# Moving the two-input elementwise operations of a decoder layer's two mixers and of its rotary rotation from GpSimd to VectorE

## The chip, the core and the metric

The kernel runs on one core of one Trainium2 chip. The metric is device time in microseconds (us) of one execution, smaller is better; the time of a kernel is the median of its runs. A core has TensorE (PE: matmuls; PEld is its weight load), VectorE (DVE), ScalarE (ACT), GpSimd (POOL) and SyncE (SP, which issues the DMAs here). Each engine works through its own queue of instructions in order and waits on semaphores where an instruction needs another engine's result.

## The reference

One layer of a hybrid decoder over 2048 tokens of width 1024, with 16 meta tokens ahead of them, batch 1, all float32. Cut to what matters:

```python
u = rmsnorm(h, norm_mix_w); proj = u @ w_in
gq, gk, gv, gr, glr, sq, sk, sv = split(proj)
o_gla = gla_mixer(gq, gk, gv, gr, glr, ...)     # 4 heads, dk 64, dv 128
o_swa = swa_mixer(sq, sk, sv, sinks, pos)       # 8 heads of 64, 2 kv heads, window 128
h = h + concat([o_gla, o_swa]) @ w_out
h = h + square(relu(rmsnorm(h, norm_ff_w) @ w_ff1)) @ w_ff2
out = rmsnorm(h, final_norm_w)[:, 16:]
# gla_mixer, per chunk, with b = cumsum(log_sigmoid(gate)) / 16:
A[i, j] = sum_d q[i, d] * k[j, d] * exp(b[i, d] - b[j, d])   for j <= i
o = A @ v + (q * exp(b)) @ S;   S = exp(b_last) * S + (k * exp(b_last - b)).T @ v
o = rmsnorm(o) * silu(r)
# swa_mixer: rotary on the first 16 of 64 dims of q and k, then
# softmax over meta tokens + window + a sink per head
xr = xr * cos + rot(xr) * sin
```

## The kernel before, in words

Everything large is a matmul in three passes: `mm3` (L158 to L162) multiplies high part by high part, low by high and high by low. Each weight tile is split by `split_w` (L119): a DMA into `raw`, the high part `wh` by ACT (L125), the low part `wl` by DVE (L126). The token axis is cut into four blocks of 512 columns.

The dense work is a Python generator: `in_proj` twice (projections of two blocks each, with the rotation in `rope`, L199), then `trunk` for blocks 0 and 1 (output projection and feed-forward), then `tail_pair`, a hand-ordered stage for blocks 2 and 3 that does not touch the mixers. `drive` (after each yield of the dense generator) takes one step of each of two further generators: `gla` (the gated linear attention, 16 chunks of 128 tokens) and `swa` (sliding-window attention, 16 blocks of 128 queries). The mixers thus run beside the matmuls of `in_proj` and `trunk`. Ahead of `tail_pair` the order in which instructions stand on each engine is set by a scheduler from these streams and the tile pools; it is not written out by hand.

A GLA chunk (`gla_chunk`) turns the gates into a running sum `B` (DVE scan, L580), makes `qkp = q*k` (L695) and from it the diagonal `dg`, spreads that into `AT` (four POOL instructions, L705), and then goes through seven levels of block sizes 64 to 1. A level (`gla_level`) makes `E = B - B[at the block's middle]` (L659), two exponentials of its halves on ACT (L660, L661), the scaled keys `kl` (L663) and the scaled queries `ql` (DVE, L667). `gla_level_mm` multiplies them into PSUM (`lv`, L677, four matmuls with the weight loads counted apart) and copies the wanted entries into `AT` (DVE, L682). There are two `E`, two `kl` and two `ql` buffers. After the levels come `qB = q*exp(B)` (L717), the decayed keys `kt` (L587 to L589, in the second `kl` buffer), the state update, and the gate `sg` of the output (L762).

The attention takes scores in PSUM tiles `sc` (two buffers, tag `sx`, shared with transposes and norms), DVE adds the mask and takes the maximum (L471, which also writes `sst`), ACT takes exponentials (L479), POOL divides by the sum (L494), PE transposes (L510), POOL masks two tiles (L523), PE multiplies by the values (L530, `pv`).

The rotation in `rope` swaps rows by a DVE shuffle into `sw` (L203), multiplies `sw` by the sine (L204), `raw` by the cosine (L205) and adds (L206); the feature is then stored by a DMA on the SP queue (L246).

The functions that the diff touches and what calls them:

Of the kernel before, what the change touches and what calls it, by code (L numbers as in the profile page):

```python
# [13 lines left out]
ALU = mybir.AluOpType  # L14
# [3 lines left out]
P = 128  # L18
# [17 lines left out]
class Layer:  # L36
# [162 lines left out]
    def rope(self, sp, raw, cs, n):  # L199

        nc = self.nc
        sw = sp.tile([P, NB], F32, name="sw", tag="sw", bufs=1)[:, :n]
        nc.vector.stream_shuffle(sw, raw, [(q + 8) % 16 if q < 16 else q for q in range(32)])  # L203
        nc.gpsimd.tensor_tensor(sw, sw, cs[:, 1, :], ALU.mult)  # L204
        nc.vector.tensor_tensor(raw, raw, cs[:, 0, :], ALU.mult)  # L205
        nc.vector.tensor_tensor(raw, raw, sw, ALU.add)  # L206
# [376 lines left out]
    def decayed_keys(self, gp, B, k, n):  # L583

        nc = self.nc
        kt = self.kl[1][:, :, :n]
        nc.gpsimd.tensor_tensor(kt, B[:, :, n - 1 : n].to_broadcast([P, 2, n]), B, ALU.subtract)  # L587
        nc.scalar.activation(kt, kt, AF.Exp, scale=1.0 / 16.0)
        nc.vector.tensor_tensor(kt, kt, k, ALU.mult)  # L589
        return kt  # L590
# [55 lines left out]
    def gla_level(self, li, gp, B, k):  # L646
        nc = self.nc
# [3 lines left out]
        def view(t):  # L651
            return t.rearrange("p a (n two s) -> p (a n) two s", two=2, s=s)


        flat = lambda t: t.rearrange("p a (n w) -> p (a n) w", w=2 * s)
        c = flat(B)[:, :, s - 1 : s].to_broadcast([P, 2 * nb, 2 * s])
        E = gp.tile([P, 2, P], F32, name="E", tag="E", bufs=2)
        Ev = view(E)
        nc.gpsimd.tensor_tensor(flat(E), flat(B), c, ALU.subtract)  # L659
        nc.scalar.activation(Ev[:, :, 0, :], Ev[:, :, 0, :], AF.Exp, scale=-1.0 / 16.0)  # L660
        nc.scalar.activation(Ev[:, :, 1, :], Ev[:, :, 1, :], AF.Exp, scale=1.0 / 16.0)  # L661
        kl = self.kl[li % 2]
        nc.gpsimd.tensor_tensor(view(kl)[:, :, 0, :], view(k)[:, :, 0, :], Ev[:, :, 0, :], ALU.mult)  # L663
        ql = gp.tile([P, 2, 2, 64], F32, name="ql", tag="ql", bufs=2)
# [22 lines left out]
    def gla_chunk(self, b, gp, qk, v):  # L687
        nc = self.nc
# [5 lines left out]
        qkp = gp.tile([P, 2, P], F32, name="qkp", tag="E", bufs=2)  # L694
        nc.gpsimd.tensor_tensor(qkp, q, k, ALU.mult)  # L695
        yield
# [19 lines left out]
        qB = gp.tile([P, 2, P], F32, name="qB", tag="qB", bufs=1)  # L716
        nc.gpsimd.tensor_tensor(qB, q, eB, ALU.mult)  # L717
        kt = self.decayed_keys(gp, B, k, P)
# [26 lines left out]
        for hp in range(2):  # L745
            for h in range(2):
                rr = slice(64 * h, 64 * h + 64)
                c = hp * 256 + h * P
# [12 lines left out]
        nc.scalar.activation(sg, sg, AF.Exp)  # L761
        nc.gpsimd.tensor_tensor(sg, sg, rf, ALU.mult)  # L762
        yield
# [916 lines left out]
```

## Time and profile before

| | |
|---|---|
| median of 3 runs | 2222.23 us (2220.12 to 2222.93) |
| profiled execution | 2224.15 us, of which the span from first to last instruction is 2222.1 us |
| granted TensorE clock, mean | 0.992 |
| ACT busy | 1049.8 us, 47% of the span, 2156 instructions |
| POOL busy in 40 slices of 55.6 us | 2042232644433344443310000000000000000001 |
| DMA | 291.47 MB, 131 GB/s mean |
| core's largest POOL group | L659, 112 instructions, 86.1 us |

How to read it: busy is the time in which an engine had an instruction running; the share of it in the span is an average over stages that differ. The slices show where in the span an engine works: POOL does nearly all of its work in the first 21 of 40 slices, which is where the two mixers run, that is up to about 1150 us. Only the last two normalisations use it after that.

In a group's row the numbers behind the bar are the busy time of the group, the mean duration of one instruction in ns, the idle time of the engine ahead of them, and what ended it. In a row of the timeline stand the start in us, the duration in us, engine, line, operation, output<-inputs, and, in brackets, how long the engine had been idle before and what released it. A row of a table of stages has the stretch, its length, and per engine the busy us with the count of instructions, then the granted clock (1.00 is full), the share of the DMA engines and GB/s.

### The profile page before, as it was taken

To read this page: it belongs to the slowest core of one execution; us is meant where nothing else is said; L and a number is where in the kernel's file an instruction comes from. 1 tells how busy PE (TensorE), PEld (TensorE's weight loads), DVE (VectorE), ACT (ScalarE), POOL (GpSimd) and SP (SyncE) were. 2 spreads that over 40 slices of the span, in tenths; PEclk is the share of its full clock that TensorE was granted. 3 is DMA by queue.
4 is the path that set the end of the run, shared out by engine and by line. 5 is a ranking of instruction groups with operands and counts; after the bars stand their busy time and mean duration, and the time that the engine had idled before them with its cause. 6 is when DMAs were issued, how large, how long until landed. Compare 5 with 4: busy or idle time off the path is not lost.

```text
span 2222.1 us, 29409 instructions
## 1 busy us (share of the span) xinstructions
PE 2160.2 (97%) x10423; PEld 1808.9 (81%) x10423; DVE 1530.8 (69%) x2617; ACT 1049.8 (47%) x2156; POOL 432.8 (19%) x621
## 2 busy tenths in 40 slices
PE   8999999989999999999999999999999999999997
PEld 6997789778788888887788888888788887888886
DVE  6166763878877777877975445556867776775866
ACT  5133754446665555656653233443455544333434
POOL 2042232644433344443310000000000000000001
PEclk9999999999999999999999999999999999999999
DMA  6333533325233333333533333563355456744412
GB/s 203 97 102 128 157 100 105 98 88 187 88 108 103 106 106 93 98 107 104 170 95 92 102 96 111 175 197 115 127 175 169 155 182 253 266 168 146 155 42 76
DMA packets 146802, 291.47 MB, mean 131 GB/s; under 512 B 12256, under 2 KB 63968, under 8 KB 146656
## 3 DMA queue, kind: packets, MB, share of 16 engines
q1 hardware_dynamic: 146656, 289.61, 40.7%
q8 instruction: 82, 1.34, 0.2%
q14 instruction: 64, 0.52, 0.1%
HBM read 219.63 MB, written 69.86 MB: 130 GB/s over the span
## 4 chain that ended last, share of the span: by engine, by line
PE 82%; DVE 9%; ACT 3%; POOL 3%; issue 2%; DMA 1%; DVEq 0%; SPq 0%; POOLq 0%; ACTq 0%
PE psd L162 15%; PE psd L160 15%; PE psd L161 15%; PE psq L160 4%; PE psq L162 4%; PE psq L161 4%; PE psw L160 4%; PE psw L162 4%; PE psw L161 4%; PE lv L677 2%; PE psd L295 2%; PE psd L296 1%; PE psd L297 1%; PE pv L530 1%; DVE wl L126 1%
## 5 line engine op out<-in xcount | busy, mean ns | idle before, releaser
L125 ACT ACTIVATE wh<-raw 128x1024 fp32r<-128x1024 f32 (+2 forms) x190 | 199.0, 1048 | 318.7 <-PE psd L162 275.9
L126 DVE TENSOR_TENSOR wl<-raw,wh 128x1024 fp32r<-128x1024 f32 (+2 forms) x190 | 239.7, 1262 | 99.5 <-ACT wh L125 98.5
L160 PE MATMUL psd<-hid,wh 128*128 128x512 f32 x512 | 205.0, 400 | 2.0 <-ACT hid L843 2.0
L1312 POOL TENSOR_TENSOR o<-acc,rb 128x256 f32<-128x256 f32 (+1 forms) x6 | 6.5, 1108 | 1019.1 <-DVE rb L85 1007.7
L160 PE MATMUL psd<-f,wh 128*128 128x512 f32 x512 | 202.7, 396 | 0.0
L162 PE MATMUL psd<-hid,wh 128*128 128x512 f32 x512 | 200.9, 392 | 0.0
L161 PE MATMUL psd<-hid,wl 128*128 128x512 f32 x512 | 200.7, 392 | 0.0
L162 PE MATMUL psd<-f,wh 128*128 128x512 f32 x512 | 199.9, 391 | 0.0
L161 PE MATMUL psd<-f,wl 128*128 128x512 f32 x512 | 199.7, 390 | 0.0
L160 PE MATMUL psd<-u,wh 128*128 128x512 f32 x416 | 170.0, 409 | 4.1 <-DVE st L241 2.4
L162 PE MATMUL psd<-u,wh 128*128 128x512 f32 x416 | 165.9, 399 | 0.6 <-DVE u L156 0.5
L161 PE MATMUL psd<-u,wl 128*128 128x512 f32 x416 | 165.1, 397 | 1.2 <-DVE wl L126 1.0
L160 PE MATMUL psw<-bh,wh 128*128 128x512 f32 x392 | 153.2, 391 | 2.2 <-DVE su L1195 2.2
L162 PE MATMUL psw<-bl,wh 128*128 128x512 f32 x392 | 153.2, 391 | 0.0
L161 PE MATMUL psw<-bh,wl 128*128 128x512 f32 x392 | 153.1, 391 | 0.0
L161 PE MATMUL psq<-oh,wl 128*128 128x512 f32 x384 | 149.5, 389 | 0.8 <-DVE wl L963 0.8
L162 PE MATMUL psq<-ol,wh 128*128 128x512 f32 x384 | 149.7, 390 | 0.6 <-DVE ol L913 0.6
L160 PE MATMUL psq<-oh,wh 128*128 128x512 f32 x384 | 149.8, 390 | 0.0
L962 ACT ACTIVATE wh<-rw 128x1024 fp32r<-128x1024 f32 x49 | 52.0, 1061 | 150.6 <-PE psw L162 134.3
L863 DVE TENSOR_TENSOR h<-h,psd 128x512 f32<-128x512 f32 x112 | 76.5, 683 | 61.2 <-PE psd L162 61.1
L160 PEld LDWEIGHTS psd<-hid,wh 128*128 128x128 f32 x512 | 97.1, 190 | 21.8 <-ACT hid L843 2.4
L162 PEld LDWEIGHTS psd<-hid,wh 128*128 128x128 f32 x512 | 96.7, 189 | 21.1 <-DVE hid L844 0.4
(315 smaller groups left out, 5494.4 us busy)
## 6 DMA issues: line engine op xcount, KB each, us to landing
raw<-w SPq DMA_DIRECT2D x132, 512.0 KB, 3.6
b<-hops SPq DMA_DIRECT2D x49, 512.0 KB, 3.6
raw<-wo SPq DMA_DIRECT2D x32, 512.0 KB, 4.0
r<-w SPq DMA_DIRECT2D x32, 512.0 KB, 4.1
rw<-w2q SPq DMA_DIRECT2D x28, 512.0 KB, 5.5
raw<-wf SPq DMA_DIRECT2D x26, 512.0 KB, 3.7
feat<-st SPq DMA_DIRECT2D x52, 256.0 KB, 2.0
hops<-t SPq DMA_DIRECT2D x42, 256.0 KB, 5.0
```

The source lines that it names most:

```text
L125: nc.scalar.activation(wh, raw, AF.Copy)
L126: nc.vector.tensor_tensor(wl, raw, wh.bitcast(F32), ALU.subtract)
L160: nc.tensor.matmul(ps, lhsT=wh, rhs=ah, start=first, stop=False, skip_group_check=skip)
L161: nc.tensor.matmul(ps, lhsT=wl, rhs=ah, start=False, stop=False, skip_group_check=skip)
L162: nc.tensor.matmul(ps, lhsT=wh, rhs=al, start=False, stop=last, skip_group_check=skip)
L295: nc.tensor.matmul(ps, lhsT=ah, rhs=wh, start=kt == 0, stop=False)
L296: nc.tensor.matmul(ps, lhsT=ah, rhs=wl, start=False, stop=False)
L297: nc.tensor.matmul(ps, lhsT=al, rhs=wh, start=False, stop=kt == KT - 1)
L530: nc.tensor.matmul(pv, lhsT=v[:, kv, :], rhs=t, start=i == 0 and t is ph, stop=False)
L677: nc.tensor.matmul(ps[:, hp * P : (hp + 1) * P], lhsT=kl[:, hp, :], rhs=ql[:, :, hp, :], start=True, stop=True)
L863: nc.vector.tensor_tensor(hs[m], hs[m], ps, ALU.add)
L962: nc.scalar.activation(wh, src, AF.Copy)
```

## The change

Seven places change their engine from `nc.gpsimd` to `nc.vector`; nothing else changes:

```diff
 rope:          (L204)
-        nc.gpsimd.tensor_tensor(sw, sw, cs[:, 1, :], ALU.mult)
+        nc.vector.tensor_tensor(sw, sw, cs[:, 1, :], ALU.mult)
 decayed_keys:  (L587)
-        nc.gpsimd.tensor_tensor(kt, B[:, :, n - 1 : n].to_broadcast([P, 2, n]), B, ALU.subtract)
+        nc.vector.tensor_tensor(kt, B[:, :, n - 1 : n].to_broadcast([P, 2, n]), B, ALU.subtract)
 gla_level:     (L659, L663)
-        nc.gpsimd.tensor_tensor(flat(E), flat(B), c, ALU.subtract)
+        nc.vector.tensor_tensor(flat(E), flat(B), c, ALU.subtract)
-        nc.gpsimd.tensor_tensor(view(kl)[:, :, 0, :], view(k)[:, :, 0, :], Ev[:, :, 0, :], ALU.mult)
+        nc.vector.tensor_tensor(view(kl)[:, :, 0, :], view(k)[:, :, 0, :], Ev[:, :, 0, :], ALU.mult)
 gla_chunk:     (L695, L717, L762)
-        nc.gpsimd.tensor_tensor(qkp, q, k, ALU.mult)
+        nc.vector.tensor_tensor(qkp, q, k, ALU.mult)
-        nc.gpsimd.tensor_tensor(qB, q, eB, ALU.mult)
+        nc.vector.tensor_tensor(qB, q, eB, ALU.mult)
-        nc.gpsimd.tensor_tensor(sg, sg, rf, ALU.mult)
+        nc.vector.tensor_tensor(sg, sg, rf, ALU.mult)
```

On POOL stay the copies into `qpad` (L692, L693), the diagonal `AT` (L705), the division `p` (L494), the masks `ph` and `pl` (L523), twelve adds of the first norms (L94) and a quarter of the last normalisation (L1312).

The scheduler lays the streams anew: POOL goes from 433 rows to 145 (a row can stand for several like instructions), DVE from 2420 to 2716, and the order on PE, ACT and SP changes in places up to the end of the mixers.

First place: the start of the levels of one chunk, in the second `in_proj` (275 us in the trace of before). On POOL before, two mask instructions, the diagonal, two `E`, the gate `sg`, and then the first `kl` of the chunk:

```order
L523 AFFINE_SELECT ph<-ph 128x512
L523 AFFINE_SELECT pl<-pl 128x512
L705 TENSOR_SCALAR AT<-tabs,dg 128x128 x4
L659 TENSOR_TENSOR E<-B 128x256 x2
L762 TENSOR_TENSOR sg<-sg,r 128x512
L663 TENSOR_TENSOR kl_122<-qk,E 128x2x64
L717 TENSOR_TENSOR qB<-qk,eB 128x256
L663 TENSOR_TENSOR kl_123<-qk,E 128x4x32
```

On POOL now the same stretch holds the masks and the diagonal alone, and the next masks follow at once. On DVE at that place (`st` is the evacuation of a projection, `acc` the sum of squares of the next block's norm), the difference is:

```order
 L241 SCALAR_TENSOR_TENSOR st<-psd,rb 128x512
-L243 TENSOR_TENSOR st<-psd,rb 128x512
-L94 TENSOR_TENSOR acc<-acc,sq 128x512
-L667 TENSOR_TENSOR ql<-qpad,E 128x256
-L94 TENSOR_TENSOR acc<-acc,sq 128x512
+L659 TENSOR_TENSOR E<-B 128x256
+L243 TENSOR_TENSOR st<-psd,rb 128x512
+L659 TENSOR_TENSOR E<-B 128x256
+L663 TENSOR_TENSOR kl_122<-qk,E 128x2x64
+L667 TENSOR_TENSOR ql<-qpad,E 128x256
+L663 TENSOR_TENSOR kl_123<-qk,E 128x4x32
 L667 TENSOR_TENSOR ql<-qpad,E 128x256
```

The two `E` and two `kl` stand ahead of the adds into `acc`, and `sg` and `qB` of the chunk no longer stand ahead of the first `kl`: they come later in DVE's queue.

Second place: DVE in the middle of a chunk's levels, in the feed-forward of block 0 (860 us). Before:

```order
L840 SCALAR_TENSOR_TENSOR fr<-psd,rb 128x512
L682 COPY_PREDICATED AT<-lmask,lv 128x8x32
L667 TENSOR_TENSOR ql<-qpad,E 128x256
L126 TENSOR_TENSOR wl<-raw,wh 128x1024
L844 TENSOR_TENSOR hid<-fr,hid 128x512
L863 TENSOR_TENSOR h<-h,psd 128x512
```

Now:

```order
L682 COPY_PREDICATED AT<-lmask,lv 128x8x32
L663 TENSOR_TENSOR kl_123<-qk,E 128x16x8
L667 TENSOR_TENSOR ql<-qpad,E 128x256
L126 TENSOR_TENSOR wl<-raw,wh 128x1024
L844 TENSOR_TENSOR hid<-fr,hid 128x512
L863 TENSOR_TENSOR h<-h,psd 128x512
L682 COPY_PREDICATED AT<-lmask,lv 128x16x16
L663 TENSOR_TENSOR kl_122<-qk,E 128x32x4
```

The `kl` of a level stands behind the `AT` copy of two levels earlier, directly ahead of its `ql`, and ahead of the split `wl` of the next weights.

Third place: DVE in the rotation, again the second `in_proj` (395 us). Before, the two products and the sum of one feature, with attention's `sst` and score rows between them:

```order
L203 STREAM_SHUFFLE sw<-st 128x512
L482 TENSOR_TENSOR sst<-sst 128x4
L486 TENSOR_TENSOR p<-p 128x4x128
L205 TENSOR_TENSOR st<-st,cs 128x512
L483 RECIPROCAL sst<-sst 128x4
L471 ISA p,sst<-sc,tabs 128x272
L471 ISA sst 128x1
L206 TENSOR_TENSOR st<-st,sw 128x512
```

Now:

```order
L486 TENSOR_TENSOR p<-p 128x4x128
L204 TENSOR_TENSOR sw<-sw,cs 128x512
L205 TENSOR_TENSOR st<-st,cs 128x512
L483 RECIPROCAL sst<-sst 128x4
L471 ISA p,sst<-sc,tabs 128x272
L471 ISA sst 128x1
L206 TENSOR_TENSOR st<-st,sw 128x512
```

The sine product `sw` (L204) stands on DVE ahead of the cosine product, so that the sum (L206) has both its inputs from its own engine.

## Prediction

> **What bounds the kernel now.** I read the page first, then a table of stages, then PE's waits, then the timeline at the longest of them. The page says that PE is busy nearly all the time:
>
> ```profile
> PE 2160.2 (97%) x10423; PEld 1808.9 (81%) x10423; DVE 1530.8 (69%) x2617; ACT 1049.8 (47%) x2156; POOL 432.8 (19%) x621
> ```
>
> The span leaves about 62 us in which PE does nothing. Since no matmul is added or removed, a gain can only come out of PE's waits and out of stretches with a low clock. The change touches the mixers, so I cut 45 to 1150 us into stages:
>
> ```profile
> core 0: us, PE busy (x) PEld busy (x) DVE busy (x) ACT busy (x) POOL busy (x), PEclk, DMA share, GB/s
> 250.00:500.00 250.00, 235.35 (x1297) 205.29 (x1296) 176.08 (x374) 120.05 (x331) 106.45 (x152) 0.98 0.34 105
> ...
> sum 1105.00, PE 1071.89 PEld 913.20 DVE 805.10 ACT 573.19 POOL 406.96; mean PE 214.38 PEld 182.64 DVE 161.02 ACT 114.64 POOL 81.39
> ```
>
> In the five stages together PE is busy 1071.9 of 1105 us, so 33 us are idle, 15 of them between 250 and 500 us. DVE works 805.1 us (73%), POOL 407 us. DVE is the fuller of the two engines, but it does not set the end by its sum. Whom PE waits for between 45 and 1200 us (total, times, longest):
>
> ```profile
> PE sc L469 <- DVE sst L471: 13.9, 11, 2.8
> PE lv L677 <- POOL kl L663: 6.8, 4, 3.4
> PE trm L501 <- DVE sst L471: 3.5, 1, 3.5
> ```
>
> 24 of the 33 us: 6.8 are POOL's, in four waits; 17.4 are DVE's, nearly all for the row that takes a score tile out of PSUM. So the question is whether POOL's waits go, and what DVE's do when it gets POOL's work.
>
> **The waits, place by place.** The longest wait for POOL, first on DVE, then POOL, then PE:
>
> ```profile
> 270.40 0.68 DVE L241 SCALAR_TENSOR_TENSOR st<-psd,rb 128x512 f32<-128x512 f32 x1
> ...
> 273.74 1.45 DVE L667 TENSOR_TENSOR ql<-qpad,E 128x256 f32<-128x256 f32 x1 [1.47 <-POOL E L659]
> ```
>
> ```profile
> 272.48 1.19 POOL L659 TENSOR_TENSOR E<-B 128x256 f32<-128x256 f32 x2
> 273.63 1.27 POOL L762 TENSOR_TENSOR sg<-sg,r 128x512 f32<-128x512 f32 x1
> 274.86 0.64 POOL L663 TENSOR_TENSOR kl<-qk,E 128x128 f32<-128x128 f32 x1
> ```
>
> ```profile
> 275.55 0.71 PE L677 MATMUL lv<-ql,kl 128*128 128x128 f32 x4 [3.41 <-POOL kl L663]
> ```
>
> Three things are seen. `E` starts on POOL at 272.48, though DVE was through with `B` and an evacuation at 270.40 + 0.68 = 271.08. Then `sg` (1.27) runs ahead of the `kl` that PE needs. And `ql`, which started in the shadow of `sg`, took 1.45 us where its kind takes half a microsecond: the two held each other. In the new order `E` follows that evacuation and `sg` comes later: 1.4 + 1.27 = 2.7 of the 3.41 us go. The Trainium skill (SBUF — State Buffer, section Who interferes with whom) says that a two-input DVE instruction and a GpSimd instruction that reads SBUF exclude each other for a whole instruction, whoever starts first. The long `ql` agrees.
>
> A wait for DVE with POOL behind it:
>
> ```profile
> 399.92 1.20 DVE L206 TENSOR_TENSOR st<-st,sw 128x512 f32<-128x512 f32 x1 [2.54 <-POOL sw L204]
> ```
>
> ```profile
> 401.67 0.39 PE L469 MATMUL sc<-kr,qs 128*128 128x272 f32 x1 [2.81 <-DVE sst L471]
> ```
>
> DVE's sum waited 2.54 us for POOL's sine product, and PE's scores waited behind it. Now the product is DVE's own, 0.6 us by the spacing of starts below, and an `E` of about 0.35 stands ahead: 2.54 - 0.6 - 0.35 = 1.6 us go. The next is a wait that mostly stays:
>
> ```profile
> 470.81 1.49 DVE L667 TENSOR_TENSOR ql<-qpad,E 128x256 f32<-128x256 f32 x1
> ```
>
> ```profile
> 473.40 0.27 PE L501 MATMUL trm<-tabs,p 128*64 128x128 f32 x1 [3.50 <-DVE sst L471]
> ```
>
> `ql` loses the excess of 1.49 over about 0.42, but a sine product of 0.6 comes in: 0.5 goes. The second wait for `kl`:
>
> ```profile
> 864.42 1.43 POOL L663 TENSOR_TENSOR kl<-qk,E 128x128 f32<-128x128 f32 x1
> ```
>
> ```profile
> 864.08 1.46 DVE L126 TENSOR_TENSOR wl<-raw,wh 128x1024 fp32r<-128x1024 f32 x1 [2.52 <-ACT wh L125]
> ```
>
> ```profile
> 865.90 0.71 PE L677 MATMUL lv<-ql,kl 128*128 128x128 f32 x4 [2.13 <-POOL kl L663]
> ```
>
> `kl` sat behind POOL's queue and was then held beside DVE's split `wl`, which had itself waited 2.52 us for ACT. In the new order `kl` stands ahead of that `wl`, so it is ready before the wait: all 2.13 go. The other two waits for `kl` are 6.8 - 3.41 - 2.13 = 1.3 us together; I take half, 0.6.
>
> Sum of waits: 2.7 + 1.6 + 0.5 + 2.1 + 0.6 = 7.5 us.
>
> **The clock behind a wait.** After three of these waits the granted clock is about half (third figure from the end) for 3.4 us:
>
> ```profile
> 276.20:279.70 3.50, 3.50 (x10) 2.76 (x9) 3.50 (x5) 1.03 (x3) 3.08 (x5) 0.52 0.62 204
> 402.40:405.80 3.40, 3.40 (x13) 2.72 (x12) 3.24 (x9) 2.86 (x13) 1.57 (x3) 0.53 0.10 33
> ...
> 866.60:870.00 3.40, 3.40 (x11) 2.60 (x10) 2.62 (x7) 2.06 (x6) 2.47 (x5) 0.53 0.53 164
> ```
>
> Each costs 3.4 x 0.47 = 1.6 to 1.7 us, 4.9 in sum. With waits of 0.7, 1.2 and 0 us left I count all three as gone. The Trainium skill (TensorE: Matmul & The Clock Gate, section HAM oscillation — how this bites in real kernels) puts the danger at idle gaps over about 3.4 us. By that rule only the first of the three dips hangs on its gap, and the sum would gain 1.7 here instead of 4.9. The rows speak against it: gaps of 2.8 and 2.1 us were followed by the half clock too.
>
> **What DVE gets.** The moved groups, and among them the largest one that stays (L494):
>
> ```profile
> L659 POOL TENSOR_TENSOR E<-B 128x256 f32<-128x256 f32 x112 | 86.1, 775 | 105.2 <-DVE ql L667 47.7 <-DVE B L580 37.6 <-DVE sst L483 7.8
> L663 POOL TENSOR_TENSOR kl<-qk,E 128x128 f32<-128x128 f32 x112 | 71.3, 639 | 58.2 <-PE lv L677 36.5 <-PE trm L501 9.3 <-ACT E L660 5.5
> L494 POOL TENSOR_SCALAR p<-p,sst 128x128 f32<-128x128 f32 x128 | 68.1, 549 | 173.7 <-DVE sst L483 153.3 <-ACT u L155 5.6 <-ACT E L660 5.1
> L204 POOL TENSOR_TENSOR sw<-sw,cs 128x512 f32<-128x512 f32 x20 | 34.0, 1702 | 47.7 <-DVE sw L203 45.0 <-issue 2.7
> ...
> L762 POOL TENSOR_TENSOR sg<-sg,r 128x512 f32<-128x512 f32 x16 | 23.3, 1454 | 113.5 <-ACT sg L761 113.5
> ...
> L695 POOL TENSOR_TENSOR qkp<-qk 128x256 f32<-128x256 f32 x16 | 16.3, 1016 | 13.7 <-DVE ql L667 4.8 <-DVE sst L476 2.8 <-ACT acc L90 2.2
> L717 POOL TENSOR_TENSOR qB<-qk,eB 128x256 f32<-128x256 f32 x16 | 12.2, 765 | 0.0
> L587 POOL TENSOR_TENSOR kl<-B 128x256 f32<-128x256 f32 x16 | 10.9, 680 | 17.5 <-PE lv L677 16.9
> ```
>
> And DVE's own rows of the same shapes:
>
> ```profile
> L667 DVE TENSOR_TENSOR ql<-qpad,E 128x256 f32<-128x256 f32 x112 | 60.5, 543 | 14.8 <-POOL E L659 7.9 <-ACT E L661 6.8
> ...
> L243 DVE TENSOR_TENSOR st<-psd,rb 128x512 f32<-128x512 f32 x44 | 30.3, 688 | 30.4 <-PE psd L162 29.4 <-DMA raw<-wf 0.7
> L205 DVE TENSOR_TENSOR st<-st,cs 128x512 f32<-128x512 f32 x20 | 29.2, 1458 | 0.1
> ...
> L206 DVE TENSOR_TENSOR st<-st,sw 128x512 f32<-128x512 f32 x20 | 16.1, 807 | 7.6 <-POOL sw L204 6.5 <-POOL E L659 0.4
> ...
> L589 DVE TENSOR_TENSOR kl<-kl,qk 128x256 f32<-128x256 f32 x16 | 7.2, 452 | 4.7 <-ACT kl L588 4.7
> ...
> L1334 DVE TENSOR_TENSOR acc<-acc,psd 128x256 f32<-128x256 f32 x16 | 6.6, 415 | 0.5 <-PE psd L162 0.5
> ...
> L393 DVE TENSOR_TENSOR vd<-vr,vd 128x128 fp32r<-128x128 f32 x15 | 4.8, 322 | 0.8 <-ACT vd L392 0.6
> ```
>
> No row shows a moved operation on DVE, so each is priced by the nearest row. `E` by 415 ns (L1334, same shape, no POOL beside it): 112 x 0.415 = 46.5. `kl` by 322 ns (`vd`, same size, two inputs in SBUF): 36.1. `sw` and `sg` by 688 ns (L243): 36 x 0.688 = 24.8. `qkp`, `qB` and `kt` by 452 ns (L589): 48 x 0.452 = 21.7. Sum 129.1; the upper end, with `E` by 543 (L667), `kl` by 452, `sw` and `sg` by 807 (L206), is 60.8 + 50.6 + 29.1 + 21.7 = 162.2. Durations overlap, though:
>
> ```profile
> 266.25 0.69 DVE L94 TENSOR_TENSOR acc<-acc,sq 128x512 f32<-128x512 f32 x1
> 266.85 0.69 DVE L85 SCALAR_TENSOR_TENSOR rb<-nt,ny 128x512 f32<-128x512 f32 x1
> ```
>
> Two instructions of 0.69 us start 0.60 apart, so each costs the queue 0.08 to 0.09 less; 308 of them 24.6 less.
>
> Against it stands what POOL no longer disturbs: the cosine product, which always ran beside the sine product, 20 x (1.458 - 0.688) = 15.4; `ql` 112 x (0.543 - 0.415) = 14.3; the sum 20 x (0.807 - 0.688) = 2.4. Relief 32.1; half of it as one end (POOL's staying work disturbs on), twice as the other (splits and adds were held too).
>
> DVE's net: 129.1 - 24.6 - 32.1 = 72.4 us, ends 40 and 121 (162.2 - 24.6 - 16). That is 805 to 877 of 1105 us, still with 228 us idle. It lies beside PE's work except where PE waits for DVE anyway: 17.4 less places two and three (2.81 + 3.50) is 11.1 us. I let these grow as the ratio of busy to idle does, 2.68 to 3.85, a factor of 1.44: 4.8 us more; 2.3 and 10.3 at the ends. This scaling is the softest term.
>
> A rule speaks against the change: by the SBUF section of the Trainium skill named above POOL's staying work reads SBUF as well and goes on holding DVE, and now 308 more instructions can be held. As an estimate, moved groups are 254 of POOL's 407 us, the other 153 are 14% of 1105; 14% of 308 is 43 hits of half an L494 (0.27), 12 us on DVE. By it the growth would be 6 us instead of 4.8, and the time 1 us more.
>
> Of the waits that come with the moved work, `kl`'s for ACT's exponential stands directly ahead of `ql`, which had it already; `E` waits for DVE's own `B`; `sg` waits for ACT, and behind it queue score rows and splits. ACT's waits for `E` shorten, off the path. POOL's remaining queue only gets shorter, and SP's stores of features come when their sum is done. From 1150 us on the engines do the same as before.
>
> **Sum.** -7.5 - 4.9 + 4.8 = -7.6 us. The profiled execution was 2224.15 us and would be 2216.5; the median is 1.9 lower: 2222.23 - 7.6 = **2214.6 us**.
>
> **Rivals.** *A draw (0.18).* The places are eased, but DVE's growth sits at its upper end, 10.3, and one new wait brings one dip, 1.6: -12.4 + 11.9 = -0.5, that is 2221.7. For it: PE's order is laid anew, so the new order has waits of its own. Against: DVE keeps 228 us idle. Within 0.2%, 4.4 us, is about what a measurement of this kernel can tell from no change.
>
> *Slower (0.32): waits move into DVE's queue.* POOL's `kl` and `kt` waited 36.5 + 16.9 = 53.4 us for PE's `lv` (rows L663, L587), and that idleness held nobody else. On DVE the score rows queue behind, and PE has two score tiles. If a third reaches PE, 17.8 us, with four dips at 1.6 and the growth of 4.8, it is 17.8 + 6.4 + 4.8 - 12.4 = +16.6: 2238.8. It decides from 7.6 us on, a seventh of the 53.4. Against: `kl` stands behind the `AT` copy that waited for the same `lv` already. For: that holds for `kl`, not for `kt` or `sg`.
>
> *Much faster.* All of POOL's 6.8, half of DVE's 17.4 and four dips go and nothing comes: -22, 2200. Part of the forecast's side.
>
> **How the numbers follow.** Forecast side 0.50, draw 0.18, slower 0.32. Range 2199 to 2239: from the full gain to the slower rival.
>
> **What would show it.** Right: no PE wait for `kl` above 1 us, full clock at 276, 402 and 867 us, the cosine product near 0.69 us, DVE's sum over the stages near 877 us. Wrong: PE's waits for `sst` above 25 us, DVE idle for PE `lv` or ACT at `kl`, `kt` or `sg`, or more half-clock stretches than before.

## The result and the profile after

| | before | after |
|---|---|---|
| median | 2222.58 us (2220.12 to 2225.27, 4 runs) | 2188.4 us (2186.58 to 2190.38, 4 runs) |
| profiled execution, its span | 2224.15, 2222.1 us | 2190.38, 2188.7 us |
| granted clock, mean | 0.992 | 0.994 |

The ratio is 0.9846, 95% interval 0.9829 to 0.9863: 34.2 us faster, where 7.6 were forecast. The direction was right, and the time lies below the forecast's range. The first part of the page of after answers to the one line shown of before:

```profile
PE 2149.2 (98%) x10423; PEld 1804.3 (82%) x10423; DVE 1575.0 (72%) x2927; ACT 1047.6 (48%) x2156; POOL 193.7 (9%) x311
```

The span fell by 33.4 us. PE's idle time fell from 2222.1 - 2160.2 = 61.9 to 2188.7 - 2149.2 = 39.5 us, which is 22.4 of it; PE's busy time fell by 11.0 for the same matmuls; the mean clocks above account for some 4.6 us of that (0.008 of 2222.1 against 0.006 of 2188.7, an estimate), and the rest is not attributed. DVE is busier by 44.2 us in the whole program. The table of stages, with the second stage and the five as one stretch:

```profile
core 0: us, PE busy (x) PEld busy (x) DVE busy (x) ACT busy (x) POOL busy (x), PEclk, DMA share, GB/s
250.00:500.00 250.00, 244.97 (x1374) 214.85 (x1373) 198.34 (x485) 130.62 (x360) 45.10 (x73) 1.00 0.38 118
...
45.00:1150.00 1105.00, 1093.92 (x5740) 934.79 (x5739) 870.62 (x2055) 585.49 (x1525) 173.04 (x283) 1.00 0.38 115
```

PE now idles 11 of 1105 us instead of 33, at a granted clock of 1.00 over the whole stretch in this execution. Whom it still waits for between 45 and 1200 us:

```profile
PE kT L596 <- DVE kl L589: 4.8, 3, 3.0
PE lv L677 <- DVE ql L667: 1.0, 1, 1.0
PE pv L530 <- POOL ph L523: 1.0, 1, 1.0
PE oT L766 <- DVE o L739: 0.9, 1, 0.9
PE sc L469 <- DVE sst L471: 0.6, 2, 0.4
```

The waits for `kl` and for the masked term (`trm`) are gone; the waits for the score rows went from 13.9 us in 11 to 0.6 in 2. No step of the forecast had that: it let the score waits outside its places grow with DVE's load. The one new wait of more than 1 us is for the decayed keys, 4.8 us in three.

The moved groups on DVE, and two that stayed there:

```profile
L667 DVE TENSOR_TENSOR ql<-qpad,E 128x256 f32<-128x256 f32 x112 | 49.0, 438 | 0.0
L659 DVE TENSOR_TENSOR E<-B 128x256 f32<-128x256 f32 x112 | 46.3, 427 | 0.6
...
L663 DVE TENSOR_TENSOR kl<-qk,E 128x128 f32<-128x128 f32 x112 | 34.2, 305 | 1.0 <-ACT E L660 0.8
...
L204 DVE TENSOR_TENSOR sw<-sw,cs 128x512 f32<-128x512 f32 x20 | 14.3, 714 | 0.1
L205 DVE TENSOR_TENSOR st<-st,cs 128x512 f32<-128x512 f32 x20 | 14.2, 710 | 0.0
...
L762 DVE TENSOR_TENSOR sg<-sg,r 128x512 f32<-128x512 f32 x16 | 11.2, 702 | 1.9 <-ACT sg L761 1.9
...
L587 DVE TENSOR_TENSOR kl<-B 128x256 f32<-128x256 f32 (+1 forms) x17 | 7.8, 461 | 0.0
L717 DVE TENSOR_TENSOR qB<-qk,eB 128x256 f32<-128x256 f32 x16 | 7.6, 476 | 0.0
...
L695 DVE TENSOR_TENSOR qkp<-qk 128x256 f32<-128x256 f32 x16 | 7.4, 460 | 0.1
```

The seven moved groups sum to 128.8 us, against 129.1 forecast. DVE's net is 44.2, so 84.6 us came off elsewhere: 24.6 by the overlap of neighbours, as worked out in the prediction, and 60 by shorter instructions in the groups that stayed, where 32.1 were forecast. The three groups that the forecast named give 28.7 of the 60 by their rows (`ql` 60.5 to 49.0, cosine product 29.2 to 14.2, sum 16.1 to 13.9); the rest is spread over groups that it left out, the splits `wl` the largest of them.

What no view quoted in the prediction showed is ACT. In the profile of before, between 45 and 1200 us, first ACT's waits and then DVE's:

```profile
ACT E L660 <- POOL E L659: 122.8, 73, 6.2
```

```profile
DVE wl L126 <- ACT wh L125: 66.3, 43, 23.9
```

In after the same two rows are:

```profile
ACT E L660 <- DVE E L659: 76.9, 39, 9.0
```

```profile
DVE wl L126 <- ACT wh L125: 43.4, 34, 23.9
```

ACT stood 122.8 us in front of the exponential of `E`. A split `wh` can stand behind that wait in ACT's queue, and DVE's `wl` needs `wh`. Of DVE's waits for `wh` over 0.3 us in the timelines of before, 15, together 22.8 us, are for a `wh` ahead of which ACT last stood idle for `E`; in after it is one, of 0.7 us. The second wait for `kl` in the prediction is such a place; ACT's rows there are:

```profile
862.07 0.31 ACT L660 ACTIVATE E<-E 128x128 f32<-128x128 f32 x1 [3.23 <-POOL E L659]
...
863.01 1.04 ACT L125 ACTIVATE wh<-raw 128x1024 fp32r<-128x1024 f32 x1
```

The exponential waited 3.23 us for `E`, `wh` came out of ACT behind it, `wl` waited 2.52 us for `wh`, and the `kl` that ran beside `wl` is the one for which PE waited 2.13 us. That a score row was late by this link too is read at no place here; it is argued from the fall of both waits.

A second place of before shows POOL's work holding DVE ahead of a score row. On DVE, POOL, ACT and PE:

```profile
1092.19 1.21 DVE L126 TENSOR_TENSOR wl<-raw,wh 128x1024 fp32r<-128x1024 f32 x1
1093.32 1.10 DVE L94 TENSOR_TENSOR acc<-acc,sq 128x512 f32<-128x512 f32 x1
1094.34 1.47 DVE L126 TENSOR_TENSOR wl<-raw,wh 128x1024 fp32r<-128x1024 f32 x1
...
1096.07 0.41 DVE L667 TENSOR_TENSOR ql<-qpad,E 128x256 f32<-128x256 f32 x1
1096.41 0.43 DVE L471 CUSTOM_DVE_ANT_0 p<-sc,tabs 128x272 f32<-128x272 f32 x1
```

```profile
1092.43 1.44 POOL L659 TENSOR_TENSOR E<-B 128x256 f32<-128x256 f32 x1 [1.98 <-DVE ql L667]
1093.84 0.90 POOL L663 TENSOR_TENSOR kl<-qk,E 128x128 f32<-128x128 f32 x1
1096.65 0.61 POOL L659 TENSOR_TENSOR E<-B 128x256 f32<-128x256 f32 x1 [1.92 <-DVE ql L667]
```

```profile
1097.30 0.32 ACT L660 ACTIVATE E<-E 128x128 f32<-128x128 f32 x1 [2.86 <-POOL E L659]
...
1097.73 1.05 ACT L125 ACTIVATE wh<-raw 128x1024 fp32r<-128x1024 f32 x1
```

```profile
1096.90 0.39 PE L469 MATMUL sc<-kr,qs 128*128 128x272 f32 x1 [2.37 <-DVE sst L471]
```

`E` starts on POOL only when DVE's `ql` is through with an earlier `E`; its exponential follows 0.8 us after `ql`, and `wh` begins behind 2.86 us of standing still, of which that 0.8 is the way over POOL. Before it an `E` and a `kl` held DVE's add into `acc` (1.10 where its kind takes 0.69) and the second split (1.47 for 1.21), so the score row behind them starts some 0.7 us later, and PE waited 2.37 us for it.

### The profile page after: what moved, and what is told of

Read it like the earlier page. It is cut to its first block, busy times and chain, and to the rows that moved or that the text cites. A ratio compares the mean times of both kernels' runs of the same rounds, so it can differ in the third digit from the quotient of the medians.

```text
span 2188.7 us, 29186 instructions
## 1 busy us (share of the span) xinstructions
PE 2149.2 (98%) x10423; PEld 1804.3 (82%) x10423; DVE 1575.0 (72%) x2927; ACT 1047.6 (48%) x2156; POOL 193.7 (9%) x311
## 4 chain that ended last, share of the span: by engine, by line
PE 84%; DVE 8%; ACT 4%; DMA 2%; issue 1%; POOL 0%; DVEq 0%; SPq 0%; ACTq 0%; POOLq 0%
PE psd L161 15%; PE psd L160 15%; PE psd L162 15%; PE psq L160 4%; PE psq L161 4%; PE psq L162 4%; PE psw L160 4%; PE psw L162 4%; PE psw L161 4%; PE lv L677 2%; PE psd L295 2%; PE psd L296 2%; PE psd L297 2%; PE pv L530 1%; ACT p L479 1%
## 5 line engine op out<-in xcount | busy, mean ns | idle before, releaser
L126 DVE TENSOR_TENSOR wl<-raw,wh 128x1024 fp32r<-128x1024 f32 (+2 forms) x190 | 233.9, 1231 | 75.3 <-ACT wh L125 74.4
L160 PE MATMUL psd<-u,wh 128*128 128x512 f32 x416 | 169.2, 407 | 4.9 <-DVE st L241 3.2
L162 PEld LDWEIGHTS psd<-f,wh 128*128 128x128 f32 x512 | 96.1, 188 | 21.1 <-DVE f L156 0.4
```

Of the source, the lines that this page charges most:

```text
L126: nc.vector.tensor_tensor(wl, raw, wh.bitcast(F32), ALU.subtract)
L160: nc.tensor.matmul(ps, lhsT=wh, rhs=ah, start=first, stop=False, skip_group_check=skip)
L162: nc.tensor.matmul(ps, lhsT=wh, rhs=al, start=False, stop=last, skip_group_check=skip)
```

## The experiments

Three theories went into the first runs. H: the engines hold each other at SBUF, and held DVE instructions delay the score rows. Q: what other engines wait for came late out of POOL's one queue. O: the scheduler's new order is simply better. Later ones are A (the lateness of `E` alone, by way of ACT) and D (the price of DVE's time). "Gain" is the difference of medians to 2222.58 us. A ratio compares a run with runs of before that were timed beside it (their medians lie between 2222.29 and 2223.6), so it need not be the quotient of the two medians shown.

### One part alone (runs 1 to 3, 9, 10) and all but one (11)

Run 1 moves `E` and `kl`; its edit, and those of the others in the same manner:

```diff
-        nc.gpsimd.tensor_tensor(flat(E), flat(B), c, ALU.subtract)
+        nc.vector.tensor_tensor(flat(E), flat(B), c, ALU.subtract)
-        nc.gpsimd.tensor_tensor(view(kl)[:, :, 0, :], view(k)[:, :, 0, :], Ev[:, :, 0, :], ALU.mult)
+        nc.vector.tensor_tensor(view(kl)[:, :, 0, :], view(k)[:, :, 0, :], Ev[:, :, 0, :], ALU.mult)
```

> Of the seven moved places only the two of the GLA levels (E and kl, 224 of 308 instructions, 157 of 254 us of the moved POOL time) go to VectorE. Three theories of the 34 us. H (the two engines hold each other at SBUF, and every held VectorE instruction delays the score rows behind it): the gain follows the POOL time that goes, 157 of 254, so 34 x 0.62 = 21 us: 2201. Q (what others wait for came late out of POOL's one queue, in which the levels' E and kl stood behind sg, AT and masks): PE's four waits for kl, ACT's waits for E and DVE's for E go, nearly the whole gain: 2192 to 2197, and the rotation's share is small. O (the scheduler's new order of DVE and ACT is luckier, whatever engine does the work): no proportion, anything from 2190 to 2225.

Run 2 moves only the sine product:

```diff
-        nc.gpsimd.tensor_tensor(sw, sw, cs[:, 1, :], ALU.mult)
+        nc.vector.tensor_tensor(sw, sw, cs[:, 1, :], ALU.mult)
```

> Only the rotation's sine product (20 large ones, 34 us of POOL) goes to VectorE. H: the cosine product always ran beside it and lost 15 us; it goes back to about 0.7 us each; these held instructions stand in the two in_proj stages alone; gain 15 of 32 us of holding, up to 10 us: 2212 to 2216. Q: DVE's 6.5 us of waiting for sw goes, and with it the wait of 2.8 us of PE at about 401 us: gain 5: 2217. O: no rule.

Run 3 moves the four others (`kt`, `qkp`, `qB`, `sg`), with lines such as:

```diff
-        nc.gpsimd.tensor_tensor(qB, q, eB, ALU.mult)
+        nc.vector.tensor_tensor(qB, q, eB, ALU.mult)
```

> Only kt, qkp, qB and sg go to VectorE (64 instructions, 63 us of POOL); E, kl and sw stay. H: 63 of 254 us, a quarter of the gain: 2214. Q: sg and qB no longer stand ahead of kl in POOL's queue, so the two long waits for kl (3.4 and 2.1 us) and their dips shrink: 2213 to 2216. Together with the other two parts the three gains add up to about 34 us by H and to less by Q, since each part alone leaves other late results.

Run 9 has only the first pair of run 1's lines (`E`), run 10 only the second (`kl`):

> The kernel before with E alone (L659) on VectorE; kl and all else stay on GpSimd. A (E is late out of GpSimd: ScalarE stands still in front of E's exponential, the splits wh queued behind it come late, VectorE waits for wh at wl, and the score rows queued behind that are late): E carries the levels' gain, 12 to 22 us, so 2200 to 2210 us, ScalarE's waits for E fall from 122.8 to about 80 us and VectorE's for wh at wl from 66.3 to about 45. H (held instructions): E is 86.1 of the 157.4 us that GpSimd loses by E and kl together, so about 12 of their 22 us: 2207 to 2213, with the waits for wh about as before.

> The kernel before with kl alone (L663) on VectorE. A: E is as late as before, so ScalarE's waits for it stay near 120 us and VectorE's for wh near 65; only TensorE's own waits for kl (6.8 us) and a little clock go: 3 to 9 us, 2213 to 2220. H: by GpSimd's time about 10 us, 2210 to 2215.

Run 11 is after, with this pair turned back:

```diff
-        nc.vector.tensor_tensor(flat(E), flat(B), c, ALU.subtract)
+        nc.gpsimd.tensor_tensor(flat(E), flat(B), c, ALU.subtract)
```

> The changed kernel with E alone (L659) put back on GpSimd. A: most of the levels' gain is lost: ScalarE's waits for E go back from 76.9 to about 110 or more, VectorE's for wh from 43.4 to about 60, and the time to 2200 to 2212 us. H: 86 us of long two-input work return to GpSimd, with VectorE relieved of 46 us and held by some 15 to 25: 2192 to 2202 us. If it is at 2188 or below, E on VectorE was worth nothing once the others were moved.

| run | median us | ratio, interval | gain us | DVE busy against before, us |
|---|---|---|---|---|
| 1 `E`, `kl` | 2200.5 | 0.9894 (0.9877 to 0.9911) | 22.1 | +39.7 |
| 2 `sw` | 2212.07 | 0.9949 (0.9932 to 0.9965) | 10.5 | -1.8 |
| 3 the four others | 2207.95 | 0.9926 (0.9906 to 0.9945) | 14.6 | +9.7 |
| 9 `E` | 2204.5 | 0.9911 (0.9895 to 0.9928) | 18.1 | +31.0 |
| 10 `kl` | 2216.42 | 0.9959 (0.9943 to 0.9974) | 6.2 | +14.8 |
| 11 all but `E` | 2193.27 | 0.9857 (0.984 to 0.9873) | 29.3 | +17.8 |

Every part gains by itself, though DVE gets busier by up to 39.7 us. Parts 1, 2 and 3 sum to 47.2, more than the whole 34.2, so they share. H's figures fit runs 1 and 2; run 3 gained more than H or Q gave it, and neither H's sum of the three (34) nor Q's (less) came true. `E` alone is worth 18.1, more than half of the whole; put on last, behind all the others, it adds only 2193.27 - 2188.4 = 4.9, and the ratio intervals of run 11 and after overlap. `sw` is the cleanest: DVE's time hardly changes (the sine product comes in, and the cosine product falls from 1458 to 772 ns), and 10.5 us go. The run does not tell the sine product's lateness (DVE's sum waited 6.5 us for it in before) from the holding of the cosine product, since both went, and the order is laid anew. Of A's expectations, those of runs 9 and 10 came true; run 9's waits are:

```profile
ACT E L660 <- DVE E L659: 84.7, 45, 7.8
```

```profile
DVE wl L126 <- ACT wh L125: 45.6, 36, 23.9
DVE E L659 <- POOL kl L663: 10.2, 12, 2.0
```

With `E` alone moved DVE's waits for `wh` are nearly where after has them, and DVE waits for POOL's `kl` instead, 10.2 us. In run 10 ACT's waits for `E` stay at 114.1, and `kl`, now on DVE, waits 13.7 us there for the late exponential, where after has 0.8. For run 11 A was wrong by 7 us: ACT's waits for `E` go back to 101.2, but the time loses 4.9, and H's figure held. DVE is 26.4 us less busy there, which may pay for part of the lateness.

### GpSimd time that nobody waits for (runs 4, 5, 6)

Products on POOL into a scratch tile behind five of the seven moved operations (not `E` and `kt`): 756 of 56 columns (run 4), 720 of 112 columns (run 5), and one product with four to eight memsets at each place (run 6). The order on PE, DVE and ACT is that of after. Run 5's lines at one place and the helper:

```diff
-        nc.vector.tensor_tensor(qB, q, eB, ALU.mult)
+        nc.vector.tensor_tensor(qB, q, eB, ALU.mult); extra_work(self, qB[:, 0, :112], 5)
+def extra_work(self, s, n):
+    for _ in range(n):
+        self.nc.gpsimd.tensor_tensor(self.extra, s, s, ALU.mult)
```

> The changed kernel with work added on POOL whose result nobody uses: at each moved place (but E and kt) three to five two-input products of 56 columns, tied in time to the moved operation's result, 756 in all, some 200 us by the 218 ns of a 16-column one and more for 56. The order on PE, DVE, ACT and SP is row for row that of the changed kernel. H: the holding comes back, two-input DVE instructions beside it lengthen (ql from 0.43 to 0.5 us and more, the sine and cosine products too), and most of the gain goes: 2205 to 2220. Q: nobody waits for the added work, but p, AT and the masks stand behind it: at most 2196. O: 2188, since the order is the same.

> The changed kernel with extra products on GpSimd that nobody uses: 112 columns each, two inputs in SBUF, four behind each kl and each large sw, three behind qkp, five behind qB, four behind sg. They are twice as wide as in the run before, so that each holds longer. The order on TensorE, VectorE, ScalarE and SyncE is that of the changed kernel. H (the two engines hold each other where they read SBUF, and the held VectorE instructions delay the score rows): the cosine product and ql lengthen again towards 1458 and 543 ns, and the time goes back by half of the gain or more, to 2205 to 2225 us. Q (what other engines wait for came late out of GpSimd's queue): nothing that they wait for stands in that queue but the masks, AT and the division, so the time rises by no more than these come later, to 2192 to 2200 us. O (the new order alone is better): about 2190 to 2194 us, however long VectorE is held.

> The changed kernel with the same kind of extra GpSimd time, but of memsets that read nothing: one product of 56 columns at each place, and six behind kl, eight behind sw, qB and sg, four behind qkp of memsets of 56 columns. Order elsewhere as in the changed kernel. H: almost nothing, since only the one product at each place can hold VectorE: 2188 to 2192 us. Q: the masks, AT and the division come as late as GpSimd's time says, as in the run with reads: 2192 to 2198 us. If it is at the time of the run with 56-column reads (2194.6), that run's 6 us were GpSimd's queue; if at the changed kernel's 2188.4, they were the holding.

Measured: 2194.56 (ratio 0.9871, 0.9854 to 0.9887), 2209.19 (0.993, 0.9915 to 0.9945) and 2190.46 us (0.9849, 0.9834 to 0.9864). The pages of runs 5 and 6:

```profile
PE 2154.9 (98%) x10423; PEld 1805.2 (82%) x10423; DVE 1618.4 (73%) x2927; ACT 1049.6 (48%) x2156; POOL 567.5 (26%) x1031
```

```profile
PE 2150.0 (98%) x10423; PEld 1803.9 (82%) x10423; DVE 1580.2 (72%) x2927; ACT 1048.1 (48%) x2156; POOL 427.0 (19%) x1643
```

Run 6 gives POOL as much to do as before had (432.8 us); of what was added 169.2 us are memsets and 73.2 us products that read. It is 2.1 us slower than after, which the intervals do not tell from nothing: POOL's queue by itself, with what is left in it, is not it. Run 5 costs 20.8 us, and DVE, with no instruction more, is busy 43.4 us longer, most of all in `E`, 427 ns in after's row above and 497 in run 5's:

```profile
L659 DVE TENSOR_TENSOR E<-B 128x256 f32<-128x256 f32 x112 | 54.2, 497 | 0.6
```

So holding is real and costs up to 20.8 / 43.4 = 0.48 us of time for each us of DVE (run 4: 16.1 us more on DVE, 6.2 more time, 0.38). It is an upper figure: in run 5 3.0 us of DVE's waits (`kl` is overwritten only when the products have read it) and 2.0 of PE's (for `p`) name POOL itself. H's time held in run 5 but not in run 4, where Q's "at most 2196" fits, and H named the wrong instructions: in run 5 the cosine product is at 747 ns and `ql` at 460, far from 1458 and 543. The Trainium skill (SBUF — State Buffer, section Who interferes with whom) has the two engines excluding each other where a VectorE instruction reads two inputs from SBUF and GpSimd reads SBUF; the memsets, which only write, agree by contrast. O falls as the whole cause: with after's order kept, 20.8 of the 34.2 us went away.

### The price of DVE's time (runs 7, 8, 14, 15)

Runs 7 (on before) and 8 (on after) add five products of 56 columns on DVE behind each `ql` and each large sum of the rotation:

```diff
-        nc.vector.tensor_tensor(raw, raw, sw, ALU.add)
+        nc.vector.tensor_tensor(raw, raw, sw, ALU.add); n > 16 and extra_work(self, raw[:, :56], 5)
```

> The kernel before, with products on VectorE that nobody uses: five of 56 columns behind each ql and behind each large sum of the rotation, about 660 instructions and 50 to 90 us, so VectorE's sum over the five stages goes from 805 to some 855 to 895 us with GpSimd's work left where it was. It measures the term of the forecast by itself. By the forecast's scaling, TensorE's waits for VectorE grow by the ratio of busy to idle time, from 17.4 to about 25 us or more, and the time goes up by 5 to 15 us, to 2228 to 2238. If load is harmless, and only instructions that were held or that waited for GpSimd made the score rows late, the waits stay at 15 to 20 us and the time within 3 us of 2222.6. The scheduler lays the order anew here, so a difference of under 5 us says nothing.

> The changed kernel with the same extra products on VectorE (five of 56 columns behind each ql and each large sum of the rotation); its sum over the five stages goes from about 871 to some 920 to 960 of 1105 us. By the forecast's scaling, busy to idle goes from 3.7 to between 5 and 6.6, so waits for VectorE of 1 to 5 us grow by no more than 4 us, while a queueing rule with a knee would give more: 2195 to 2215 us. If load is harmless as long as nothing in VectorE's queue is held or waits for GpSimd, 2187 to 2193 us.

Runs 14 (on before) and 15 (on after) leave out half of the columns or heads of five DVE instructions that both kernels have, so what they compute is no longer the layer. One of the five places:

```diff
-        nc.vector.tensor_tensor(raw, raw, cs[:, 0, :], ALU.mult)
+        w = n // 2; nc.vector.tensor_tensor(raw[:, :w], raw[:, :w], cs[:, 0, :w], ALU.mult)
```

> The kernel before with VectorE work left out that both kernels have: the copies into AT for two of four heads, the cosine product and the sum of the rotation for half of the columns, the sums of squares for half of the columns, and half of the product for the decayed keys; about 50 us of VectorE's 805 in the five stages, no instruction more or less, GpSimd's work as it was. Theory D (VectorE's time costs 0.4 to 0.66 us per us here, as the added work showed): 2190 to 2205 us. By the forecast's scaling (0.07 us per us) 2218 to 2222 us.

> The changed kernel with the same VectorE work left out: about 50 us of 871. D: 2155 to 2170 us, and then the change's 65 us more on VectorE cost some 25 to 40 us and what GpSimd's part in the chain had cost is 60 us or more. By the forecast's scaling (busy to idle 3.7 to 2.9): 2183 to 2188 us. If it gains much less than the kernel before does by the same cut, load costs where GpSimd is in the chain and not elsewhere.

The pages of runs 8 and 15:

```profile
PE 2165.5 (98%) x10423; PEld 1809.3 (82%) x10423; DVE 1658.3 (75%) x3587; ACT 1047.6 (47%) x2156; POOL 198.1 (9%) x311
```

```profile
PE 2141.6 (99%) x10423; PEld 1799.5 (83%) x10423; DVE 1523.8 (70%) x2927; ACT 1051.0 (48%) x2156; POOL 190.2 (9%) x311
```

| run | median us | ratio, interval | time us | DVE busy us | us per us |
|---|---|---|---|---|---|
| 7 before, more | 2275.54 | 1.0235 (1.0218 to 1.0252) | +53.0 | +134.0 | 0.40 |
| 8 after, more | 2218.03 | 0.9973 (0.9962 to 0.9984) | +29.6 | +83.3 | 0.36 |
| 14 before, less | 2209.81 | 0.9938 (0.9923 to 0.9953) | -12.8 | -50.1 | 0.25 |
| 15 after, less | 2175.86 | 0.9786 (0.9772 to 0.9801) | -12.5 | -51.2 | 0.24 |

No expectation held in the four runs: the forecast's scaling (0.07) is far too low, and D's 0.4 to 0.66 too high for work taken away. Added or held work costs 0.36 to 0.48, work taken away in both kernels alike gives 0.24 to 0.25; why they differ was not tried. The price of a us of DVE is about the same in before and after, so load costs the same with POOL's two-input work there or gone. That work makes the load itself larger, though: the same 660 products keep DVE busy 134.0 us longer in before and 83.3 in after (behind `ql` 310 and 224 ns each). The scheduler lays the order anew in these four runs, which is a caveat to each.

### `E` late, and the same work with nobody waiting (runs 12, 13)

Run 12 sends `E` through a POOL step before its exponential (the hop):

```diff
-        nc.vector.tensor_tensor(flat(E), flat(B), c, ALU.subtract)
+        nc.vector.tensor_tensor(flat(E), flat(B), c, ALU.subtract); nc.gpsimd.tensor_scalar(E[:, 0], E[:, 0], 1.0, None, ALU.mult)
```

> The changed kernel with a step on GpSimd behind E: E is computed on VectorE, then half of it is multiplied by 1 in place on GpSimd (one input, 128x128), and the exponentials wait for that. Nothing else is changed; TensorE's order is nearly that of the changed kernel. It makes E late by 0.6 us and more without the two-input work on GpSimd. A: ScalarE's waits for E go from 76.9 to 110 us or more and the time to 2196 to 2215 us. H: some 60 us more of one-input GpSimd time, which by the run with memsets and the one with 56-column reads costs 2 to 4 us: 2190 to 2193 us.

Run 13 has such a step behind `ql`, for nobody:

```diff
-        )
+        ); nc.gpsimd.tensor_scalar(self.extra, ql[:, 0].rearrange("p a b -> p (a b)")[:, :112], 1.0, None, ALU.mult)
```

> The changed kernel with the hop's GpSimd step where nobody waits for it: behind each ql, 112 columns of it are multiplied by 1 into a scratch tile (one input, 112 instructions). The order on all other engines is that of the changed kernel. A (E's lateness itself costs the time of the run with the hop): 2188 to 2192 us, so that 7 us or more of that run's 10.3 are the lateness. H (GpSimd's reading costs it, whoever waits): about 2196 to 2199 us.

Measured: 2198.72 us (0.988, 0.9865 to 0.9895) with the hop, 2189.01 (0.985, 0.9833 to 0.9866) without a reader. ACT's waits in runs 12 and 13:

```profile
ACT E L660 <- POOL E L659: 114.3, 63, 7.0
```

```profile
ACT E L660 <- DVE E L659: 78.6, 40, 9.0
```

POOL's busy time is nearly the same in both (263.1 and 267.8 us) and DVE's too (1576.2 and 1578.1). So 2198.72 - 2189.01 = 9.7 us are the lateness of `E` alone (6.7 by the two ratios, whose intervals just touch). Run 13 has after's order on PE, DVE and ACT, run 12 differs from it in places, which is a caveat. That a late `E` costs time by way of its exponential on ACT is shown. How the lateness then comes to DVE is not what A said. DVE's waits for the exponential in runs 12 and 13:

```profile
DVE kl L663 <- ACT E L660: 18.0, 19, 1.8
```

```profile
DVE kl L663 <- ACT E L660: 0.7, 2, 0.5
```

DVE's waits for `wh` grow only from 43.2 to 50.0. In run 12 the lateness thus reaches DVE mostly through `kl`, which in before stood on POOL, and less through the splits. The hop's 37.4 us more of ACT waiting are most of the 45.9 us that the change took away. Scaled by that, the change's own share is about 9.7 x 45.9 / 37.4 = 12 us, 8 by the ratios: an estimate that takes the two ways to DVE as equally dear, which no run shows.

### What is left on POOL (runs 16, 17, 18)

Run 16 puts `sg` and `qB` back, with lines such as:

```diff
-        nc.vector.tensor_tensor(sg, sg, rf, ALU.mult)
+        nc.gpsimd.tensor_tensor(sg, sg, rf, ALU.mult)
```

> The changed kernel with sg (L762) and qB (L717) back on GpSimd, whose results few wait for, and with E and kl not behind them any more. D: VectorE is relieved of 19 us, held by some 5 to 8 more, so it gains 3 to 8 us: 2180 to 2186 us. H: 36 us of long two-input work hold VectorE again, for about the same as the relief: 2187 to 2193 us. Q in its first form (each result out of GpSimd is late and is waited for): 2192 to 2200 us.

Run 17 moves the diagonal `AT` to DVE, run 18 to ACT:

```diff
-            nc.gpsimd.tensor_scalar(AT[:, h, :], self.ident, dg[:, h : h + 1], 1.0, ALU.mult, ALU.mult)
+            nc.vector.tensor_scalar(AT[:, h, :], self.ident, dg[:, h : h + 1], 1.0, ALU.mult, ALU.mult)
```

```diff
-            nc.gpsimd.tensor_scalar(AT[:, h, :], self.ident, dg[:, h : h + 1], 1.0, ALU.mult, ALU.mult)
+            nc.scalar.activation(AT[:, h, :], self.ident, AF.Copy, scale=dg[:, h : h + 1])
```

> The changed kernel with the diagonal AT (L705, 64 instructions of one input) on VectorE too. VectorE gets 64 instructions of 0.15 to 0.35 us, 10 to 22 us, which at the price of 0.25 us per us costs 2 to 6 us; against it GpSimd reads 42 us less. If holding by one-input GpSimd work matters, 2184 to 2188 us; if only VectorE's time counts, 2190 to 2195 us.

> The changed kernel with the diagonal AT (L705) on ScalarE as a scaled copy. VectorE gets nothing and is held less, ScalarE gets some 64 x 0.25 = 16 us, with the splits wh and the exponentials of E behind it. If GpSimd's staying work still costs, 2182 to 2187 us; if ScalarE's queue is what matters (as E's lateness did), 2188 to 2194 us.

Run 16: 2192.97 us (0.9864, 0.9849 to 0.9879), 4.6 slower than after. DVE's busy time is 1577.3, not less than after's 1575.0: what the two would have saved on DVE they took by holding. D's guess was wrong: it took the holding for 5 to 8 us, and it is about 18.8 + 2.3 = 21, an estimate (11.2 and 7.6 from after's rows, and the difference of the two busy times); the time fits H's upper end. Run 17: 2184.69 us (0.9829, 0.9816 to 0.9843); run 18: 2188.39 (0.9841, 0.9828 to 0.9855). The group in the two:

```profile
L705 DVE TENSOR_SCALAR AT<-tabs,dg 128x128 f32<-128x128 f32 x64 | 15.1, 296 | 0.0
```

```profile
L705 ACT ACTIVATE AT<-tabs,dg 128x128 f32<-128x128 f32 x64 | 20.7, 389 | 3.2 <-DVE dg L702 3.2
```

The diagonal on DVE is the fastest of the full kernels, 3.7 us below after. The two were not timed side by side and their ratio intervals overlap, so that gain is likely rather than shown. The order changes with it: PE's waits for the decayed keys are 1.2 us there instead of 4.8, which may be the gain. On ACT it gains nothing: either the relief of POOL is spent again on ACT's queue, as the expectation had it, or neither counts; the run does not tell these apart.

## Why the prediction was wrong in size

**What held.** The cost of the moved work on DVE, 129.1 forecast and 128.8 measured, and each of its four terms within 2 us. All four waits for `kl` went, and the granted clock is full between 45 and 1150 us in the profiled execution. Of the score wait at 401.67 at most 0.4 is left, where 1.2 was allowed. At 275.55 1.0 us of the 3.41 stays, under a new name, where 0.7 was allowed. `sg` and its neighbours no longer stand ahead of the chunk's first `kl`. The signs that were to show the forecast right came, DVE's sum over the stages (870.6) and the cosine product (0.71 us) too; none of them looked at ACT or at the other score waits, so they could not show what it missed.

**What failed: the sum's view of where the gain could come from.** The forecast took its relief, 12.4 us, from five places and three clock dips where the profile names POOL on PE's wait or one step behind it, and called PE's other 11.1 us of waits for DVE a matter of DVE's load, which would grow to 15.9 ("I let these grow as the ratio of busy to idle does"). The score waits went to 0.6, and the wait for `trm`, of which 0.5 of 3.50 us was to go, went whole. Two further stretches of half clock, at 474 and 1037 us, which the sum did not count, went as well. The waits fell while DVE's load rose, so that load by itself had not made them. What POOL did to DVE and ACT had a part, as the runs show: the instructions it held (60 us of DVE, forecast 32.1; run 5 gives holding its price), the sine product on POOL (run 2, 10.5 us with DVE's time nearly unchanged, late or holding) and the lateness of `E` by way of ACT (run 12 against 13). The sentence "ACT's waits for `E` shorten, off the path" is the plainest miss: a late `E` costs 9.7 us in run 12, and in before a split `wh`, and DVE's `wl` with it, waited behind it.

**The load term was wrong too, in the other direction.** The forecast charged 4.8 us for a net of 72.4 us on DVE. The net was 44.2, since twice as much holding went away as taken, within the ends given (40 to 121). But the price is 0.24 to 0.48 us per us (runs 5, 8, 15) and not 0.07, so 44.2 us cost some 11 to 21, an estimate. Two errors of opposite sign: the relief is then 34.2 + 11 to 34.2 + 21, 45 to 55 us instead of 12.4.

**Where those 45 to 55 us are** is separated only in part. About 12 are the lateness of `E` by the estimate above, with its reserve. `kl` alone gave 6.2, `sw` alone 10.5 and the four others 14.6, each net of what it put on DVE. The parts sum to 47.2 by themselves and to 34.2 together, so no single list of shares exists, and the shares of holding, of lateness, of the clock and of the new order stay open.

**The slower rival.** Its mechanism did not come: POOL's 53.4 us of waiting for `lv` did not move to DVE, which idles 1.0 us ahead of `kl` and 0.0 ahead of `kt` by the rows above, and the score waits fell. What came is another wait, for `kt` itself. In after, on PE, ACT and DVE:

```profile
425.36 0.41 PE L596 MATMUL kT<-tabs,kl 128*128 128x128 f32 x2 [2.99 <-DVE kl L589]
```

```profile
423.77 0.42 ACT L588 ACTIVATE kl<-kl 128x256 f32<-128x256 f32 x1 [2.76 <-DVE kl L587]
```

```profile
423.33 0.41 DVE L587 TENSOR_TENSOR kl<-B 128x256 f32<-128x256 f32 x1
423.66 1.21 DVE L126 TENSOR_TENSOR wl<-raw,wh 128x1024 fp32r<-128x1024 f32 x1
424.80 0.41 DVE L589 TENSOR_TENSOR kl<-kl,qk 128x256 f32<-128x256 f32 x1
```

`kt` comes late in DVE's queue, and its product stands behind a split. Its price is 4.8 us in three waits, below the 7.6 from which the rival would have decided. The rival "much faster" had the right side, 2200, and was still 11.6 us short. The draw needed PE's waits for DVE to grow by 10.3 us; the score waits fell, and the new ones do not reach that.

**The rule against the change** (POOL's staying work goes on holding DVE) is borne out in kind, and small: with the diagonal off POOL and nothing put on DVE (run 18) DVE is busy 3.3 us less, 1571.7 for 1575.0, and the time is the same. The forecast's extra charge for it was 1 us.

## What to carry to other kernels

When an engine with its own queue hands results to others, read the waits of every engine for it, not only those of the bound one: here ACT stood 122.8 us in front of `E`, on no view of PE's waits, and a late `E` by itself cost 9.7 us. Price an engine's load by an experiment that widens or narrows instructions it has anyway; a ratio of busy to idle time gave 0.07 where the runs gave 0.24 to 0.48. And moving work onto the busier engine can pay, as here, where the slower one took twice as long for it (254 us against 128.8), held the busier one meanwhile, and was waited for.

## What the runs showed of the hardware

- A gap of PE was not always followed by a low clock. After has one of 2.99 us at 425.36, and the stretch round it stays at full clock, where before had half after gaps of 2.81 and 2.13 us. In run 13, which has after's order on PE, the same matmul waits the same 2.99 us, and half the clock follows for 3.4 us. So the length of a gap does not decide alone; what else does was not tried. The full clock at this place of after is luck, worth some 3.4 x 0.5 = 1.7 us. The Trainium skill's limit of about 3.4 us (TensorE: Matmul & The Clock Gate, section HAM oscillation — how this bites in real kernels) agrees with after's gap and not with those of before and of run 13. First after, then run 13:

```profile
424.00:429.00 5.00, 3.64 (x19) 3.12 (x20) 5.00 (x9) 1.72 (x4) 0.64 (x1) 1.00 0.49 163
```

```profile
423.10 0.41 PE L596 MATMUL kT<-tabs,kl 128*128 128x128 f32 x2 [2.99 <-DVE kl L589]
```

```profile
424.30:427.70 3.40, 3.40 (x10) 2.63 (x9) 3.40 (x5) 0.00 (x0) 0.15 (x1) 0.50 0.82 240
```

- How much DVE is held depends on more than POOL's time. Run 13's one-input steps (267.8 - 193.7 = 74.1 us of POOL) lengthened DVE's busy time by 3.1 us, 0.04 each us; run 4's two-input ones of 56 columns (504.4 - 193.7 = 310.7 us) by 16.1, 0.05 each us; run 5's of 112 columns (373.8 us of POOL) by 43.4, 0.12 each us.
